# Short-sequence attention on one core: Q and K loaded 32 heads at a time, with the exponential putting the queries back in order

One core of one Trainium2 chip. The metric is device time in microseconds (us), median over runs.

## The reference

```python
batch, n_heads, seq, head_dim = 32, 12, 128, 64          # float32, 384 heads in all
scale = 1.0 / np.sqrt(q.shape[-1])
scores = scale * np.matmul(q, k.transpose(0, 1, 3, 2))
attn = np.exp(scores - np.max(scores, axis=-1, keepdims=True))
attn = attn / (np.sum(attn, axis=-1, keepdims=True) + 1e-8)
return np.matmul(attn, v).astype(np.float32)
```

Inputs are 3 x 12.58 MB, the output 12.58 MB: 50.33 MB must pass between HBM and SBUF whatever the kernel does.

## The kernel before

It works in 24 chunks of 16 heads. GpSimd (POOL) issues the loads, which cast float32 to bf16 on the way (36.70 MB read, 18.35 MB landed); DVE turns Q, K and the output in 32x32 blocks; ACT does the exponential; finished chunks wait nine chunks before ACT issues their stores (`LAG`), so that the loads go first. The parts that matter here:

```python
    TQ = 16; GQ = S // TQ; T = 8; A = 8; CB = 4; NCH = B * H // 16; AHEAD = 7; LAG = 9

    def runs(x, t):
        return x.rearrange("b h (g t) d -> (b h g) (t d)", t=t).rearrange(
            "(n p) x -> p n x", p=128)

    qr, kr, vr, orr = runs(q, TQ), runs(k, TQ), runs(v, T), runs(out, TQ)
    # ... cut ...
    def load_qk(c):
        for src, which in ((qr, 0), (kr, 1)):
            x = pin.tile([128, TQ, D], bf16, tag="qk"[which] + "_bf", name="qk"[which] + "_bf")
            nc.gpsimd.dma_start(out=x, in_=src[:, c, :].rearrange("p (t d) -> p t d", t=TQ))
            chunks[c, which] = x
    # ... cut ...
    def store(c, eng):
        o_sb, _ = osbs.pop(c)
        eng.dma_start(out=orr[:, c, :], in_=o_sb.rearrange("p t d -> p (t d)"))

    e = NCH - 1
    held = {c: [c - LAG] if c >= LAG else [] for c in range(e - 3)}
    held[e - 3] = [e - 12, e - 11, e - 10, e - 9]
    held[e - 2] = [e - 8, e - 7, e - 6]
    held[e - 1] = [e - 5, e - 4, e - 3]
    held[e] = [e - 2, e - 1, e]
    # ... in the loop over chunks, after the work of chunk c:
        for s in held[c]:
            store(s, nc.scalar if s < e - 2 else nc.sync)
```

A chunk's output tile is 128 partitions of 4 KB, and in HBM the chunk is 128 adjacent rows of 4 KB.

The softmax here doesn't subtract the row's maximum and nothing guards it: scores larger than these inputs give would overflow.

## Time and profile before

| | before |
|---|---|
| time | 131.46 us (130.61 to 131.75, 3 runs) |
| profiled span | 129.4 us |
| busy: PE, DVE, ACT, POOL | 56%, 67%, 55%, 61% |
| DMA engines | full in 38 of 40 slices |
| first to last data packet | 126.0 us, for 50.33 MB |

No compute engine is full, and the 16 DMA engines are. The DMA lines of the page are in the prediction below. "Under 512 B" in them counts, in this kernel, packets of 4 bytes: 1344 = 84 x 16, 16 for each DMA. For a DMA from SP or ACT I read this number as the number of engines that carry it.

### The profile page before, as it was taken

The numbers are of one execution on the slowest core, as the hardware profiler recorded it, in microseconds if no ns is written. First come the engines' busy times: TensorE is split into PE (matmuls) and PEld (weight loads), VectorE is DVE, ScalarE is ACT, GpSimd is POOL, SyncE is SP. The second block draws the span as 40 slices with busy tenths as digits, with TensorE's granted clock in tenths as the row PEclk, the third lists the DMA queues.
The fourth block names the chain that finished last, engine by engine and source line by source line (L and its number), as shares of the span: only waits on it lengthen the run. The fifth ranks groups of instructions, "written<-read, shape, count | busy, mean of one in ns | idle before, by whom it ended". The sixth has DMA issues, their size and how long they took to land.

```text
span 129.4 us, 4637 instructions
## 1 busy us (share of the span) xinstructions
PE 72.9 (56%) x2080; PEld 43.6 (34%) x2080; DVE 86.5 (67%) x150; ACT 71.3 (55%) x74; POOL 79.5 (61%) x88
## 2 busy tenths in 40 slices
PE   0049537597746763886622976460977764856000
PEld 0037335334323442354402454220642442535000
DVE  0246576658879697879944589854578999795800
ACT  3219908567948745865760857580637777335000
POOL 6933133335799986998724895909999445553500
PEclk9999976869999999599996579998555999555555
DMA  3999999999999999999999999999999999999991
GB/s 114 275 193 205 209 209 208 208 210 205 211 208 212 204 211 209 209 208 210 282 288 281 208 212 282 288 286 246 250 209 286 236 298 317 405 414 399 412 408 54
DMA packets 16723, 32.27 MB, mean 249 GB/s; under 512 B 1344, under 2 KB 7488, under 8 KB 16704
## 3 DMA queue, kind: packets, MB, share of 16 engines
q0 software_dynamic: 12960, 18.35, 79.8%
q10 hardware_dynamic: 3168, 11.54, 23.0%
q1 hardware_dynamic: 576, 2.10, 4.2%
q8 instruction: 16, 0.26, 0.7%
q14 instruction: 3, 0.02, 0.0%
HBM read 37.75 MB, written 12.58 MB: 389 GB/s over the span
## 4 chain that ended last, share of the span: by engine, by line
DMA 56%; DVE 14%; POOL 11%; PE 9%; issue 2%; ACT 1%; POOLq 0%; DVEq 0%; ACTq 0%
DMA k_bf<-in_k_dram 34%; DMA q_bf<-in_q_dram 11%; DMA v_bf<-in_v_dram 11%; DVE o_sb L178 6%; PE s_ps L120 5%; POOL o_sb L183 4%; POOL v_bf L65 4%; DVE kt L109 3%; PE o_ps L159 3%; DVE qt L107 3%; POOL q_bf L58 2%; ACT attn L124 1%; PE v_ps L139 1%; DVE o_sb L186 1%; POOL k_bf L58 1%
## 5 line engine op out<-in xcount | busy, mean ns | idle before, releaser
L124 ACT ACTIVATE attn<-s_ps 128x2048 bf16<-128x2048 f32 x24 | 45.1, 1879 | 40.6 <-PE s_ps L120 38.5
L183 POOL TENSOR_TENSOR o_sb<-o_sb,recip 128x1024 f32<-128x1024 f32 x23 | 44.0, 1915 | 9.9 <-DVE o_sb L178 9.7
L178 DVE STREAM_TRANSPOSE o_sb<-o_ps 128x512 f32<-128x512 f32 x48 | 33.3, 712 | 15.7 <-PE o_ps L159 14.8
L120 PE MATMUL s_ps<-qt,kt 32*128 32x128 bf16 x768 | 18.6, 245 | 34.2 <-DVE kt L109 34.2
L139 PE MATMUL v_ps<-v_bf,perm 128*32 128x512 bf16 (+1 forms) x448 | 35.0, 418 | 2.7 <-DMA v_bf<-in_v_dram 2.0
L120 PEld LDWEIGHTS <-kt 32*128 32x128 bf16 x768 | 13.8, 106 | 44.2 <-DVE kt L109 44.2
L143 ACT CAST v<-v_ps 128x512 bf16<-128x512 f32 x48 | 26.1, 593 | 2.1 <-PE v_ps L139 2.0
L159 PE MATMUL o_ps<-attn,v 128*32 128x128 bf16 x768 | 22.9, 251 | 1.1 <-issue 1.0
L58 POOL DMA_DIRECT2D k_bf<-in_k_dram x23 | 12.3, 535 | 15.7 <-DMA v_bf<-in_v_dram 11.6
L109 DVE STREAM_TRANSPOSE kt<-k_bf 128x512 f32<-128x512 f32 x24 | 16.4, 684 | 6.2 <-DMA k_bf<-in_k_dram 6.1
L107 DVE STREAM_TRANSPOSE qt<-q_bf 128x512 f32<-128x512 f32 x24 | 16.3, 679 | 5.5 <-DMA q_bf<-in_q_dram 5.4
L159 PEld LDWEIGHTS <-v 128*32 128x32 bf16 x768 | 16.0, 111 | 10.3 <-issue 5.2
L65 POOL DMA_DIRECT2D v_bf<-in_v_dram x12 | 9.3, 778 | 13.0 <-DMA k_bf<-in_k_dram 4.2
L171 DVE STREAM_TRANSPOSE dt<-d_ps 128x512 f32<-128x512 f32 x24 | 16.3, 680 | 1.0 <-PE d_ps L149 1.0
L149 PE MATMUL d_ps<-attn,ones 128*32 128x512 bf16 x96 | 11.2, 453 | 9.0 <-ACT attn L124 8.9
L58 POOL DMA_DIRECT2D q_bf<-in_q_dram x23 | 13.2, 576 | 3.0 <-DMA k_bf<-in_k_dram 1.3
L139 PEld LDWEIGHTS <-perm 128*32 128x32 bf16 x448 | 11.8, 114 | 6.2 <-issue 3.5
L149 PEld LDWEIGHTS <-ones 128*32 128x32 bf16 x96 | 4.4, 103 | 15.4 <-issue 13.2
L173 DVE RECIPROCAL recip<-dt 128x16 f32<-128x16 f32 x24 | 6.1, 254 | 1.9
L83 DVE CAST q_bf<-raw 128x1024 bf16<-128x1024 f32 x1 | 0.7, 694 | 5.5 <-DMA raw<-in_q_dram 5.5
L83 ACT CAST k_bf<-raw 128x1024 bf16<-128x1024 f32 x1 | 1.0, 1045 | 3.2 <-DMA raw<-in_k_dram 3.2
L83 ACT ACT_TABLE_LOAD x1 | 1.3, 1283 | 1.2 <-PEq L243 1.2
(11 smaller groups left out, 3.9 us busy)
## 6 DMA issues: line engine op xcount, KB each, us to landing
out_dram<-o_sb ACTq DMA_DIRECT2D x21, 512.0 KB, 6.8
v_bf<-in_v_dram POOLq DMA_DIRECT2D x12, 512.0 KB, 13.5
q_bf<-in_q_dram POOLq DMA_DIRECT2D x23, 256.0 KB, 12.4
k_bf<-in_k_dram POOLq DMA_DIRECT2D x23, 256.0 KB, 12.4
out_dram<-o_sb SPq DMA_DIRECT2D x3, 512.0 KB, 6.4
raw<-in_k_dram ACTq DMA_DIRECT2D x1, 512.0 KB, 4.9
raw<-in_q_dram SPq DMA_DIRECT2D x1, 512.0 KB, 4.7
```

The lines of the kernel that those rows point to most:

```text
L58: nc.gpsimd.dma_start(out=x, in_=src[:, c, :].rearrange("p (t d) -> p t d", t=TQ))
L107: nc.vector.transpose(xt.rearrange("p h (x g) -> p x h g", g=GQ), x)
L109: nc.vector.transpose(xt.rearrange("p h (x g) -> p x h g", g=GQ), x.rearrange("p (y t) e -> p t y e", y=2))
L120: nc.tensor.matmul(s_ps[:, b, h, :], lhsT=kt[pr, h, :, j], rhs=qt[pr, h, :, j], start=(j == 0), stop=(j == 1), tile_position=(b * 32, 0))
L124: nc.scalar.activation(out=attn, in_=s_ps, func=mybir.ActivationFunctionType.Exp, bias=0.0, scale=scale)
L139: nc.tensor.matmul(v_ps[u * 32:(u + 1) * 32, i], lhsT=perm[:, a + i, tl, :], rhs=v_bf[:, ns, 2 * u + tl, :], start=(tl == 0), stop=(tl == ...
L143: nc.scalar.copy(v2s[m][:, a:a + heads, ns], v_ps)
L149: nc.tensor.matmul(d_ps[b * 32:(b + 1) * 32], lhsT=ones, rhs=attns[c][:, b], start=True, stop=True, tile_position=(0, b * 32))
L159: nc.tensor.matmul(o_ps[b * 32:(b + 1) * 32, h], lhsT=v2s[c // 4][:, 4 * (b % 2) + h, 2 * (c % 4) + b // 2, j * 32:(j + 1) * 32], rhs=attn ...
L171: nc.vector.transpose(dt, turned(d_ps))
L178: nc.vector.transpose(o_sb[:, :, j * 32:(j + 1) * 32], turned(o_ps))
L183: nc.gpsimd.tensor_mul(o_sb, o_sb, recip.to_broadcast([128, TQ, D]))
```

## The change

Its intent: fewer and larger transfers. Q and K come for 32 heads (a "duo" of two chunks) in one DMA, in runs of 8 KB instead of 4 KB, and are turned with one DVE instruction for 32 heads. A partition then holds 32 queries of a head, and the exponential writes its result in another order so that an output row is again 16 queries, 4 KB. The core of the diff:

```diff
-    AHEAD = 7
+    NDUO = NCH // 2
+    AHEAD = 5
-    qr, kr, vr, orr = runs(q, TQ), runs(k, TQ), runs(v, T), runs(out, TQ)
+    qr, kr, vr = runs(q, 2 * TQ), runs(k, 2 * TQ), runs(v, T)
+    orr = out.rearrange("b h s d -> (b h s d)").rearrange(
+        "(m b i p x) -> m i b p x", m=NDUO, b=4, i=2, p=32)
 ...
+    def load_qk(m, which):
+        x = pin.tile([128, 2 * TQ, D], bf16, tag="qk"[which] + "_bf", name="qk"[which] + "_bf")
+        nc.gpsimd.dma_start(
+            out=x, in_=(qr, kr)[which][:, m, :].rearrange("p (t d) -> p t d", d=D))
 ...
+            xt = pt.tile([128, 8, S], f32, tag="qk"[which] + "t", name="qk"[which] + "t")
+            nc.vector.transpose(
+                xt.rearrange("p h (x g) -> p x h g", g=4),
+                x.rearrange("p (y t) e -> p t y e", t=(TQ, T)[which]))
 ...
-                            s_ps[:, b, h, :], lhsT=kt[pr, h, :, j], rhs=qt[pr, h, :, j],
+                            s_ps[:, b, h, :], lhsT=kt[pr, 4 * (c % 2) + h, :, j],
+                            rhs=qt[pr, 4 * (c % 2) + h, :, j],
 ...
-            nc.scalar.activation(out=attn, in_=s_ps, func=mybir.ActivationFunctionType.Exp,
-                                 bias=0.0, scale=scale)
+            nc.scalar.activation(
+                out=attn.rearrange("p b h (x g y) -> p (b h x) g y", g=4, y=2),
+                in_=s_ps.rearrange("p b h (x y g) -> p (b h x) g y", g=4, y=2),
+                func=mybir.ActivationFunctionType.Exp, bias=0.0, scale=scale)
 ...
-                        lhsT=v2s[c // 4][:, 4 * (b % 2) + h, 2 * (c % 4) + b // 2,
+                        lhsT=v2s[c // 4][:, 4 * (c % 2) + h, 4 * (c // 2 % 2) + b,
 ...
-            eng.dma_start(out=orr[:, c, :], in_=o_sb.rearrange("p t d -> p (t d)"))
+            eng.dma_start(out=orr[c // 2, c % 2], in_=o_sb.rearrange("p t d -> p (t d)"))
 ...
-            if c + AHEAD < NCH:
-                load(c + AHEAD)
+            if c % 2 == 0 and c // 2 + 6 < NDUO:
+                load_v(c // 2 + 6)
+            if c // 2 + AHEAD < NDUO:
+                load_qk(c // 2 + AHEAD, c % 2)
```

Cut: the loads ahead of the loop and their order, the first chunk's casts (twice as large), the matching pattern of `perm`, the sizes of the tile pools and the step at which a duo is turned. `store`'s tile in SBUF is the same as before; only its address pattern in HBM is new.

More of the change, by code (lines that the diff above doesn't have):

```diff
@@ L41, in runs @@
             "(n p) x -> p n x", p=128)
-    qr, kr, vr, orr = runs(q, TQ), runs(k, TQ), runs(v, T), runs(out, TQ)
+    qr, kr, vr = runs(q, 2 * TQ), runs(k, 2 * TQ), runs(v, T)
+    orr = out.rearrange("b h s d -> (b h s d)").rearrange(
+        "(m b i p x) -> m i b p x", m=NDUO, b=4, i=2, p=32)
     singles = ctx.enter_context(tc.tile_pool(name="singles", bufs=1))
-    pin = ctx.enter_context(tc.tile_pool(name="pin", bufs=AHEAD + 3))
-    pt = ctx.enter_context(tc.tile_pool(name="pt", bufs=3))
+    pin = ctx.enter_context(tc.tile_pool(name="pin", bufs=AHEAD))
+    pt = ctx.enter_context(tc.tile_pool(name="pt", bufs=2))
     pa = ctx.enter_context(tc.tile_pool(name="pa", bufs=3))
@@ L53 @@
     chunks, qts, attns, v2s, osbs = {}, {}, {}, {}, {}
-    def load_qk(c):
-        for src, which in ((qr, 0), (kr, 1)):
-            x = pin.tile([128, TQ, D], bf16, tag="qk"[which] + "_bf", name="qk"[which] + "_bf")
-            nc.gpsimd.dma_start(out=x, in_=src[:, c, :].rearrange("p (t d) -> p t d", t=TQ))
-            chunks[c, which] = x
+    def load_qk(m, which):
+        x = pin.tile([128, 2 * TQ, D], bf16, tag="qk"[which] + "_bf", name="qk"[which] + "_bf")
+        nc.gpsimd.dma_start(
+            out=x, in_=(qr, kr)[which][:, m, :].rearrange("p (t d) -> p t d", d=D))
+        chunks[m, which] = x
     def load_v(m):
@@ L69 @@
     with tc.manual_schedule():
-        early = {0: 0, 1: 1, 2: 2, 3: 3, 4: 4, 5: 5}
-        early.update({4 * m - 5 + i: 2 * m + i for m in range(3, NCH // 4) for i in range(2)})
-        def load(c):
-            load_qk(c)
-            if c in early:
-                load_v(early[c])
-        for src, which, eng, cast in ((qr, 0, nc.sync, nc.vector.tensor_copy),
-                                      (kr, 1, nc.scalar, nc.scalar.copy)):
-            raw = po.tile([128, TQ, D], f32, tag="o_sb", name="raw")
-            eng.dma_start(out=raw, in_=src[:, 0, :].rearrange("p (t d) -> p t d", t=TQ))
-            x = pin.tile([128, TQ, D], bf16, tag="qk"[which] + "_bf", name="qk"[which] + "_bf")
-            cast(x, raw)
-            chunks[0, which] = x
-        load_v(early[0])
-        load_qk(1)
+        for src, which, eng in ((qr, 0, nc.sync), (kr, 1, nc.scalar)):
+            raw = po.tile([128, 2 * TQ, D], f32, tag="raw", bufs=2, name="raw")
+            eng.dma_start(out=raw, in_=src[:, 0, :].rearrange("p (t d) -> p t d", d=D))
+            chunks[0, which] = raw
+        load_v(0)
+        load_qk(1, 0)
         ident = singles.tile([128, 128], bf16)
         make_identity(nc, ident)
-        load_v(early[1])
+        load_qk(1, 1)
+        load_v(1)
         perm = singles.tile([128, A, 2, 32], bf16)
@@ L93, with turn @@
             nc.vector.tensor_copy(
-                perm[:, :, tl, tl * 16:(tl + 1) * 16].rearrange("p a (x g) -> p a x g", x=2),
-                ident.rearrange("p (a g x) -> p a x g", a=A, x=2))
+                perm[:, :, tl, tl * 16:(tl + 1) * 16].rearrange("p a (x g) -> p a x g", x=4),
+                ident.rearrange("p (a g x) -> p a x g", a=A, x=4))
         ones = singles.tile([128, 32], bf16)
         nc.vector.memset(ones, 1.0)
-        for c in range(2, AHEAD):
-            load(c)
-        def turn(c, which):
-            x = chunks.pop((c, which)).bitcast(f32)
-            xt = pt.tile([128, 4, S], f32, tag="qk"[which] + "t", name="qk"[which] + "t")
-            if which == 0:
-                nc.vector.transpose(xt.rearrange("p h (x g) -> p x h g", g=GQ), x)
-            else:
-                nc.vector.transpose(xt.rearrange("p h (x g) -> p x h g", g=GQ),
-                                    x.rearrange("p (y t) e -> p t y e", y=2))
-            qts[c, which] = xt.bitcast(bf16).rearrange("p h (s j) -> p h s j", j=2)
+        for which in range(2):
+            raw = chunks[0, which]
+            x = pin.tile([128, 2 * TQ, D], bf16, tag="qk"[which] + "_bf", name="qk"[which] + "_bf")
+            nc.vector.tensor_copy(x[:, :TQ], raw[:, :TQ])
+            nc.scalar.copy(x[:, TQ:], raw[:, TQ:])
+            chunks[0, which] = x
+        for m in range(2, AHEAD):
+            if m == 3:
+                load_v(3)
+            load_qk(m, 0)
+            load_qk(m, 1)
+            if m == 2:
+                load_v(2)
+            if m == 3:
+                load_v(4)
+                load_v(5)
+        def turn(m, which):
+            x = chunks.pop((m, which)).bitcast(f32)
+            xt = pt.tile([128, 8, S], f32, tag="qk"[which] + "t", name="qk"[which] + "t")
+            nc.vector.transpose(
+                xt.rearrange("p h (x g) -> p x h g", g=4),
+                x.rearrange("p (y t) e -> p t y e", t=(TQ, T)[which]))
+            qts[m, which] = xt.bitcast(bf16).rearrange("p h (s j) -> p h s j", j=2)
         def scores(c):
-            qt, kt = qts.pop((c, 0)), qts.pop((c, 1))
+            qt, kt = qts[c // 2, 0], qts[c // 2, 1]
             s_ps = ps.tile([128, 4, 4, S], f32, tag="s_ps", name="s_ps")
@@ L210 @@
             todo = shuffles.get(c, [])
-            if c < e:
-                turn(c + 1, 0)
-                turn(c + 1, 1)
+            if c < e - 1:
+                turn(c // 2 + 1, c % 2)
             d_ps = denominators(c)
```

## The prediction

In the prediction and the expectations, k is the number of DMA engines that carry a DMA. That the store, with 4 as its slowest dimension in HBM, gets k = 4 is assumed there (the "rule on k"): the kernel before has 16 small packets for every DMA and doesn't show it. "Engines 0 to 3", "0 to 7" and "0 and 1" are only names for the engines that carry the stores, "4 to 15" for the rest.

> **What bounds the kernel now.** I read the strip of 40 slices first, then the DMA queues, the chain of work that ended last, the costliest groups, and the packet records of the trace. From the page of the kernel before:
>
> ```profile
> DMA  3999999999999999999999999999999999999991
> GB/s 114 275 193 205 209 209 208 208 210 205 211 208 212 204 211 209 209 208 210 282 288 281 208 212 282 288 286 246 250 209 286 236 298 317 405 414 399 412 408 54
> DMA packets 16723, 32.27 MB, mean 249 GB/s; under 512 B 1344, under 2 KB 7488, under 8 KB 16704
> ...
> q0 software_dynamic: 12960, 18.35, 79.8%
> q10 hardware_dynamic: 3168, 11.54, 23.0%
> q1 hardware_dynamic: 576, 2.10, 4.2%
> ...
> HBM read 37.75 MB, written 12.58 MB: 389 GB/s over the span
> ...
> DMA 56%; DVE 14%; POOL 11%; PE 9%; issue 2%; ACT 1%; POOLq 0%; DVEq 0%; ACTq 0%
> ```
>
> The 16 DMA engines are full from the second slice to the last but one. The GB/s row counts what lands; the casting loads land bf16, half of what they read. So 208 in slices 4 to 18, when only loads run, is 416 GB/s read, and 405 to 414 at the end, when only stores run, is the same rate. Counting the source bytes in the packet records confirms this: 411.6 GB/s over the stretch of loads alone, 407.0 where loads and stores mix, 397.2 over the last stores. The size of a piece hardly matters: two-microsecond stretches of almost only v pieces (2 KB read, 1 KB landed) run at 401 to 418, of only q/k pieces (4 KB read, 2 KB landed) at 405 to 424, of only stores (4 KB) at 391 to 426. So the kernel is bound by bytes per DMA engine: 50.33 MB / 16 engines = 3.146 MB each. First to last data packet is 126.0 us, and they begin about 3.4 us into the 129.4 us span. The timed run is 131.46 us, 2 us more than the profiled span.
>
> No compute engine comes close, and the groups that the change touches are these (busy us, mean ns | idle before):
>
> ```profile
> L124 ACT ACTIVATE attn<-s_ps 128x2048 bf16<-128x2048 f32 x24 | 45.1, 1879 | 40.6 <-PE s_ps L120 38.5
> L58 POOL DMA_DIRECT2D k_bf<-in_k_dram x23 | 12.3, 535 | 15.7 <-DMA v_bf<-in_v_dram 11.6
> L109 DVE STREAM_TRANSPOSE kt<-k_bf 128x512 f32<-128x512 f32 x24 | 16.4, 684 | 6.2 <-DMA k_bf<-in_k_dram 6.1
> L107 DVE STREAM_TRANSPOSE qt<-q_bf 128x512 f32<-128x512 f32 x24 | 16.3, 679 | 5.5 <-DMA q_bf<-in_q_dram 5.4
> ...
> out_dram<-o_sb ACTq DMA_DIRECT2D x21, 512.0 KB, 6.8
> ```
>
> DVE is busy 67% and the exponential, the largest group of ACT, sits idle 40.6 us before its instructions. A store of 512 KB lands in 6.8 us beside other traffic. Stores begin at 57.9 us, since each is held back nine chunks.
>
> [...] 58 casting loads, 22 DMAs on q10 and 4 on q1, each with 16 small packets, make 84 x 16 = 1344, which is exactly the count "under 512 B". A smaller k isn't shown by the kernel before.
> [...]
>
> **The change part by part.**
>
> *Q/K loads.* 46 casting DMAs of 128 pieces become 22, and the two first uncast ones double to 1 MB. In the packet records a 1 KB landed piece takes 98 ns and a 2 KB one 173 ns, so 75 ns per KB and 23 ns fixed; a 4 KB one is then, as an estimate, 23 + 4 x 75 = 323 ns instead of 2 x 173 = 346. In packet time that is 5888 x 173 = 1019 us against 2816 x 323 = 910 us, plus about 40 us more in the first raw loads: 69 us / 16 = 4 us at the very most. But packet times of one queue overlap (their sum is 107.7% of 16 engines' span) and the rate in bytes is the same for both sizes, so I count 0 to 1 us. The 24 fewer DMAs save 24 x 16 x 20 ns / 16 = 0.5 us of small packets.
>
> *POOL issues.* 46 x 0.555 us = 25.5 us becomes about 22 x 0.555 = 12.2 us: 13 us less on an engine that feeds a queue which is never empty. Worth 0.
>
> *Turns.* 48 DVE transposes of 512 elements at 0.68 us = 32.7 us become 24 of 1024. From the recorded 670 ns minimum[...], one takes 1.2 us, so 28.9 us: 3.8 us less on DVE, which isn't the bound. Worth 0.
>
> *Exponential.* Same 2048 elements, contiguous output, read out of order from PSUM: 1.88 us each. Even 20% more would be 9 us against 40 us of idle time. Worth 0. The first chunk's casts double (0.69 + 1.05 us more) and wait for 2 MB instead of 1 MB, about 2.6 us later: hidden behind the loads in flight.
>
> *Stores.* Here is the term that I let decide. A chunk now holds heads 4i to 4i+3 of each of four groups of eight. The output pattern goes from 128 rows of 4 KB in one even step to 4 blocks, 256 KB apart, of 32 adjacent rows of 4 KB. The blocks can't be merged with the rows, as the other chunk's 128 KB lies between them. The runs stay 4 KB, but the slowest dimension in HBM is now 4 instead of 128. [...] The loads (128 rows outermost) still use all 16.
>
> Work of each of engines 0 to 3: loads 37.75 MB / 16 = 2.359 MB, stores 12.58 MB / 4 = 3.146 MB, together 5.505 MB. One engine moves 407 / 16 = 25.4 GB/s in the mixed part. 5.505 MB / 25.4 GB/s = 216.5 us. Engines 4 to 15 have 2.359 MB, 93 us, and idle for the rest. Are engines 0 to 3 busy throughout? Until the first store at about 58 us they carry loads as now; from then one store is 131 KB / 25.4 GB/s = 5.2 us on them, plus 98 KB / 25.4 = 3.9 us of a chunk's loads, 9.0 us, while the compute produces a chunk in less than 5 us. Stores pile up, and with 12 output tiles and a lag of nine about three stores stand in the queue when the loop stalls for a free output tile. So they don't run dry. The path is: 3.4 us to the first packet, some 1 us for the ramp, 216.5, and the last receipt, about 0.5 us: 221.4 us span; with the 2 us between span and timed run 223.4. Four engines alone could go nearer to their shortest packet, 159 ns for 4 KB (25.8 GB/s), which takes about 2 us off. I predict 222 us.
>
> **The rivals.**
> *A: the store still uses all 16 engines* [...]. For it: stores come through today on 16 engines. [...] Then bytes per engine are unchanged, nothing else is on the path, and the time is 129 to 133 us.
> *B: larger pieces raise the DMA rate.* For it: 23 ns fixed per packet[...]. Against it: equal bytes per second for 1, 2 and 4 KB pieces in the records. With 16-engine stores, at most 4 + 0.5 us: about 127 us, faster by over 2%.
> *C: k is 4 but the four engines change from store to store.* For it: nothing in this profile tells engines apart. [...] Then the bytes even out, a store merely takes longer to land, and the time is 130 to 138 us.
> *D: k is 4, and engines 0 to 3 also run dry* while the loop waits for an output tile or for loads slowed on those four. For it: a store needs 9 us beside loads[...]. Against it: twelve output tiles and ten chunks of loads in flight. It would add 5 to 15 us: 227 to 237.
>
> **Range and chances.** I hold the rule on k at a little over 0.8[...]. Within it, 25.8 GB/s with perfect filling gives 218, rates a little higher on four engines alone about 210, and rival D up to 238. I don't stretch the range over the gap to A and B: 207 to 238. Slower by over 2%: 0.83 (k = 4, and a little of C). Same: 0.13 (A, part of C). Faster: 0.04 (B).
>
> **What would show each step right or wrong.** Right: "under 512 B" falls to 34 x 16 + 2 x 16 + 24 x 4 = 672; with 16-engine stores it would be 960. The GB/s row falls from about 58 us on and ends at about 100, a quarter of 408, over more than 50 us, with the DMA row at 2 or 3 tenths. A store's time to landing rises from 6.8 us to well over 10. The chain of waits names the output transfer, and DVE or POOL wait for it. Turns x24 at about 1.2 us, exponential at 1.88 us. The rate before the first store stays near 208 landed: if it rises above 215, the step on piece size is wrong. A DMA row of nines to the end, or 960 small packets, makes the whole prediction wrong.

## The result, and the profile after

| | before | after |
|---|---|---|
| time, median | 131.36 us (130.61 to 131.75, 4 runs) | 218.41 us (217.91 to 218.98, 4 runs) |
| profiled span | 129.4 us | 216.1 us |
| first to last data packet | 126.0 us | 212.7 us |

The ratio is 1.664 (95% interval 1.655 to 1.673). Ratios here are the mean time of one kernel's fast runs over that of the other's fast runs of the same rounds, so not quite the ratio of the medians quoted. Executions over 1.5% slower than the fastest of the same kernel are left out of the means.

The strip of 40 slices and the DMA queues of the kernel after, the counterpart of the first fence in the prediction:

```profile
DMA  6999999999999999952222222222222222222221
GB/s 220 274 205 218 203 216 204 213 213 210 210 213 237 231 230 244 234 128 83 77 71 71 101 109 105 109 105 106 108 106 105 106 105 106 105 106 105 106 105 67
DMA packets 12979, 32.80 MB, mean 152 GB/s; under 512 B 672, under 2 KB 6816, under 8 KB 12704
...
q0 software_dynamic: 9504, 17.83, 44.3%
q10 hardware_dynamic: 2916, 12.06, 13.9%
q1 hardware_dynamic: 540, 2.62, 3.2%
```

The slices are 5.4 us now. Until slice 17, at 92 us, all 16 engines are full, as before, for the loads still keep the other twelve busy. Then the row of nines drops to 2 tenths for half the kernel, and the rate to 105 to 106 GB/s. Four engines out of 16 are 25%, and 105 / 4 = 26.3 GB/s for each, against 407 / 16 = 25.4 in the mixed part of the kernel before: full speed for four engines, nothing for twelve. The small packets have fallen to 672 = 34 x 16 (casting loads) + 2 x 16 (first loads) + 24 x 4 (stores): four for each store. Slices 19 to 22 show less than 105 only because some loads, which land half of what they read, still run on the same four engines; counted by source bytes that stretch is at 99 to 105 GB/s.

The groups that the change touched (busy us, mean ns of one | idle before), and the issues of the stores:

```profile
L133 ACT ACTIVATE attn<-s_ps 128x2048 bf16<-128x2048 f32 x24 | 45.0, 1877 | 88.2 <-PE s_ps L128 51.1
L116 DVE STREAM_TRANSPOSE qt<-q_bf 128x1024 f32<-128x1024 f32 x12 | 14.5, 1209 | 1.4 <-DMA q_bf<-in_q_dram 1.4
L116 DVE STREAM_TRANSPOSE kt<-k_bf 128x1024 f32<-128x1024 f32 x12 | 14.4, 1203 | 0.0
L62 POOL DMA_DIRECT2D k_bf<-in_k_dram x11 | 6.4, 578 | 10.0 <-DMA v_bf<-in_v_dram 4.3
...
out_dram<-o_sb ACTq DMA_DIRECT2D x21, 512.0 KB
```

Everything that the change set out to make cheaper is as cheap as hoped. The exponential costs the same out of order (1877 against 1879 ns), 24 turns of 1.2 us replace 48 of 0.68, and half as many issues take half as long. The store's line has lost its last number: the profile gives no time to landing for these stores.

Three more views of the kernel after: the chain of waits, one line of the list of all waits (total us, times, longest us), and the timeline near the end (start us, duration us, what; an "x4" spans four instructions):

```profile
ACTq 8%; DVE 1%; ACT 1%; PE 0%; issue 0%; DVEq 0%
```

```profile
DVE o_sb L189 <- DMA out_dram<-o_sb: 42.3, 10, 11.0
```

```profile
137.22 15.70 ACTq L202 DMA_DIRECT2D out_dram<-o_sb  x4
148.61 35.23 SPq L202 DMA_DIRECT2D out_dram<-o_sb  x3
153.02 1.88 ACT L133 ACTIVATE attn<-s_ps 128x2048 bf16<-128x2048 f32 x1 [14.00 <-issue]
153.10 24.07 ACTq L202 DMA_DIRECT2D out_dram<-o_sb  x3
177.28 1.88 ACT L133 ACTIVATE attn<-s_ps 128x2048 bf16<-128x2048 f32 x1 [22.38 <-issue]
```

Issuing a store, normally half a microsecond (median 0.565 us), took up to 14.4 us: ACT sat in its issue, for what the trace doesn't show, and the exponential behind it in the same program order came 22 us late. DVE, too, waited 42.3 us for stores to leave output tiles free. This chain covers only some 10% of the span, a sign that it has lost the track: it stops at an issue that began at 160.5 us and doesn't show what that issue waited for. Read alone it would point to ACT as the culprit. E3 tests that.

### The profile page after: what moved, and what is told of

Its sections match the earlier page's. It is cut to its first block, busy times and chain, and to the rows that moved or that the text cites. A ratio compares the mean times of both kernels' runs of the same rounds, so it can differ in the third digit from the quotient of the medians.

```text
span 216.1 us, 4593 instructions
## 1 busy us (share of the span) xinstructions
PE 76.4 (35%) x2080; PEld 45.2 (21%) x2080; DVE 83.0 (38%) x127; ACT 73.0 (34%) x75; POOL 67.1 (31%) x64
## 5 line engine op out<-in xcount | busy, mean ns | idle before, releaser
L133 ACT ACTIVATE attn<-s_ps 128x2048 bf16<-128x2048 f32 x24 | 45.0, 1877 | 88.2 <-PE s_ps L128 51.1
L189 DVE STREAM_TRANSPOSE o_sb<-o_ps 128x512 f32<-128x512 f32 x48 | 32.3, 699 | 56.4 <-DMA out_dram<-o_sb 42.3
L150 PE MATMUL v_ps<-v_bf,perm 128*32 128x512 bf16 (+1 forms) x448 | 37.4, 440 | 9.8 <-DMA v_bf<-in_v_dram 8.8
L182 DVE STREAM_TRANSPOSE dt<-d_ps 128x512 f32<-128x512 f32 x24 | 16.4, 682 | 32.4 <-PE d_ps L160 32.2
L128 PE MATMUL s_ps<-qt,kt 32*128 32x128 bf16 x768 | 19.1, 244 | 26.8 <-DVE kt L116 26.3
L170 PEld LDWEIGHTS <-v 128*32 128x32 bf16 x768 | 17.0, 115 | 12.6 <-issue 8.5
L150 PEld LDWEIGHTS <-perm 128*32 128x32 bf16 x448 | 13.0, 117 | 12.4 <-issue 9.7
L116 DVE STREAM_TRANSPOSE qt<-q_bf 128x1024 f32<-128x1024 f32 x12 | 14.5, 1209 | 1.4 <-DMA q_bf<-in_q_dram 1.4
L116 DVE STREAM_TRANSPOSE kt<-k_bf 128x1024 f32<-128x1024 f32 x12 | 14.4, 1203 | 0.0
L62 POOL DMA_DIRECT2D q_bf<-in_q_dram x11 | 5.9, 540 | 17.6 <-DMA v_bf<-in_v_dram 7.5
L62 POOL DMA_DIRECT2D k_bf<-in_k_dram x11 | 6.4, 578 | 10.0 <-DMA v_bf<-in_v_dram 4.3
L197 POOL TENSOR_TENSOR o_sb<-o_sb,recip 128x512 f32<-128x512 f32 x1 | 1.0, 1044 | 21.2 <-issue 21.2
L97 ACT CAST q_bf<-raw 128x1024 bf16<-128x1024 f32 x1 | 1.0, 1045 | 6.3 <-DMA raw<-in_q_dram 6.3
```

The lines of the kernel that those rows point to most:

```text
L62: nc.gpsimd.dma_start(out=x, in_=(qr, kr)[which][:, m, :].rearrange("p (t d) -> p t d", d=D))
L116: nc.vector.transpose(xt.rearrange("p h (x g) -> p x h g", g=4), x.rearrange("p (y t) e -> p t y e", t=(TQ, T)[which]))
L128: nc.tensor.matmul(s_ps[:, b, h, :], lhsT=kt[pr, 4 * (c % 2) + h, :, j], rhs=qt[pr, 4 * (c % 2) + h, :, j], start=(j == 0), stop=(j == 1), ...
L133: nc.scalar.activation(out=attn.rearrange("p b h (x g y) -> p (b h x) g y", g=4, y=2), in_=s_ps.rearrange("p b h (x y g) -> p (b h x) g y" ...
L150: nc.tensor.matmul(v_ps[u * 32:(u + 1) * 32, i], lhsT=perm[:, a + i, tl, :], rhs=v_bf[:, ns, 2 * u + tl, :], start=(tl == 0), stop=(tl == ...
L170: nc.tensor.matmul(o_ps[b * 32:(b + 1) * 32, h], lhsT=v2s[c // 4][:, 4 * (c % 2) + h, 4 * (c // 2 % 2) + b, j * 32:(j + 1) * 32], rhs=attn ...
```

## The experiments

My theory: the store's outermost dimension of 4 puts all output through four DMA engines, and nothing else in the change matters. Rivals: blocks with gaps in HBM are slow in themselves; the 8 KB loads or the new order of compute cost the time; ACT's long issues do.

### E5 to E8: the kernel before, with only the store's pattern changed

One edit, with K = 4, 8, 16, 2. The rows land in the wrong places, so the result is wrong; the work and the bytes are the same.

```diff
-    qr, kr, vr, orr = runs(q, TQ), runs(k, TQ), runs(v, T), runs(out, TQ)
+    qr, kr, vr = runs(q, TQ), runs(k, TQ), runs(v, T)
+    orr = out.rearrange("b h s d -> (b h s d)").rearrange(
+        "(m b i p x) -> m i b p x", m=NCH // 2, b=K, i=2, p=128 // K)
-            eng.dma_start(out=orr[:, c, :], in_=o_sb.rearrange("p t d -> p (t d)"))
+            eng.dma_start(out=orr[c // 2, c % 2], in_=o_sb.rearrange("p t d -> p (t d)"))
```

> The kernel before with nothing changed but the store's address pattern in HBM: 4 blocks of 32 rows with gaps (rows land in the wrong places: a wrong result on purpose). Theory: the pattern alone makes the loss; engines 0 to 3 carry 2.359 + 3.146 = 5.505 MB at 25.4 to 26.4 GB/s, 214 to 222 us; small packets 928 + 64 of the raw loads and their queue's share as before and 24 x 4 = 96 for stores, 1056 in all. Rival (loads of 8 KB or the compute's new order share in it): under 200 us.

> The same with 8 blocks of 16 rows (wrong result on purpose). Theory: k = 8; engines 0 to 7 carry 2.359 + 1.573 = 3.932 MB, 149 to 155 us of transfer plus 6 to 7 us: 156 to 162 us. Rival (any gap in the pattern costs the same, or more blocks cost more): 218 us or more.

> The same with 16 blocks of 8 rows (wrong result on purpose). Theory: k = 16; the gaps cost nothing, 130 to 133 us, like the kernel before. Rival (gaps in HBM are the cost): slower than e6.

> The same with 2 blocks of 64 rows (wrong result on purpose). Theory: k = 2; engines 0 and 1 carry 2.359 + 6.291 = 8.650 MB, 328 to 341 us of transfer plus 6 to 7 us: 334 to 348 us. Rival (fewer, larger blocks are better for HBM): under 218 us.

| K | MB on the fullest engine | expected us | measured us | first to last data packet | GB/s of that engine | small packets |
|---|---|---|---|---|---|---|
| 2 | 8.650 | 334 to 348 | 339.06 | 333.8 us | 25.9 | 1008 |
| 4 | 5.505 | 214 to 222 | 220.12 | 215.1 us | 25.6 | 1056 |
| 8 | 3.932 | 156 to 162 | 160.99 | 155.5 us | 25.3 | 1152 |
| 16 | 3.146 | 130 to 133 | 133.16 (3 fast runs) | 127.5 us | 24.7 | 1344 |
| before | 3.146 | | 131.56 in those rounds | 126.0 us | 25.0 | 1344 |

The small packets are 928 + 32 + 24 K in every row (my text for E5 says 64 for the first loads where it is 32; its sum of 1056 was right). The GB/s rows of K = 8 and K = 2, the two profiles in turn:

```profile
GB/s 167 220 207 210 207 208 206 208 210 207 209 209 210 209 207 233 256 259 259 266 244 158 193 158 161 258 223 157 151 158 173 212 209 209 210 210 196 211 209 56
```

```profile
GB/s 198 201 208 208 209 209 208 219 220 179 96 73 116 38 95 45 104 49 53 54 52 55 53 52 52 53 52 52 54 53 52 52 52 53 52 52 52 53 52 40
```

The end plateau is about 210 for K = 8, 105 for K = 4 and 52 for K = 2: 26.2 to 26.3 GB/s per engine each time. So one line, the address pattern of the store, makes the whole loss. Bytes on the fullest engine at one rate, 25.6 GB/s, plus about 5 us before, after and outside the profiled span, give the times for K = 2, 4 and 8 within 1.5%; for K = 16 they give 128, 4% too little. Gaps in HBM as the cause of the loss are out: K = 16 has the most gaps and is nearly as fast as before. Nearly: 1.0177 (1.009 to 1.026), with fast runs from 132.70 to 134.50 us, at the edge of what I expected; by the record's limit of 2% its verdict is "unclear". The average packet of its last stores took 173 ns against 162 before (and 172 in E11, which has the same blocks), so 16 blocks of 32 KB with gaps seem a little slower to write than one run of 512 KB. Why, no run here shows.

### E3: all stores from SP

```diff
-                store(s, nc.scalar if s < e - 2 else nc.sync)
+                store(s, nc.sync)
```

> The changed kernel with all stores issued from SP instead of ACT and SP; still 4 blocks. Theory (engines 0 to 3 are full from the first store on): 216 to 220 us, though ACT no longer sits behind the issue of stores (22 us before one exponential in the changed kernel). Rival (the long issues of stores on ACT hold up the compute and so the end): 190 to 210 us.

Measured: correct, 219.8 us. The waits are quite other ones. The issues of the stores (ns min/median/max, first and last start us), and two lines of the list of waits:

```profile
L202 SPq DMA_DIRECT2D out_dram<-o_sb x24: 529/4726/13087, 32.7 to 193.1; - x24
```

```profile
ACT v L154 <- PE v_ps L150: 57.6, 16, 16.5
PE v_ps L150 <- DMA v_bf<-in_v_dram: 55.5, 6, 17.4
```

The first store is issued from SP at 32.7 us, where ACT issued it at 62.0 us, and the longest waits are now for V tiles, not ACT's for its own queue. The time is nearly the same. ACT's long issues were a symptom: with four engines full to the end, it doesn't matter which engine waits.

### E1: the same change with 16 blocks

The duo's heads are shared out to its two chunks alternately, instead of four and four of each eight. Then the block (4) and head (4) dimensions merge into one of 16.

```diff
-        "(m b i p x) -> m i b p x", m=NDUO, b=4, i=2, p=32)
+        "(m b i p x) -> m i b p x", m=NDUO, b=16, i=2, p=8)
 ...
-                            s_ps[:, b, h, :], lhsT=kt[pr, 4 * (c % 2) + h, :, j],
-                            rhs=qt[pr, 4 * (c % 2) + h, :, j],
+                            s_ps[:, b, h, :], lhsT=kt[pr, 2 * h + c % 2, :, j],
+                            rhs=qt[pr, 2 * h + c % 2, :, j],
 ...
-                        lhsT=v2s[c // 4][:, 4 * (c % 2) + h, 4 * (c // 2 % 2) + b,
+                        lhsT=v2s[c // 4][:, 2 * h + c % 2, 4 * (c // 2 % 2) + b,
```

> The changed kernel with the chunk's heads taken as 2h+i of each eight instead of 4i+h, so that the store's pattern is 16 blocks of 8 rows instead of 4 blocks of 32 rows; everything else as changed; right result. Theory [...]: k = 16, small packets 960 instead of 672, DMA row full to the end, 127 to 132 us. Rival (scattered blocks of a store are slow in themselves, or the 8 KB loads or the reordered exponential cost the time): stays above 200 us. If 8 KB loads do raise the rate (the changed kernel read about 2% more per us before its first store), it beats 131.4 by 1 to 3 us.

Measured: correct, 136.15 us, 960 small packets. The indices in four places bring back 82 us. But 136.15 is 1.036 (1.032 to 1.041) of before, and not the 127 to 132 us that I expected. Its strip, and one line each of its timeline and its waits (total us, times, longest us):

```profile
DMA  4999999999999999999999999999999859999992
GB/s 100 411 240 208 196 216 207 205 218 206 206 218 208 215 212 207 217 202 216 261 300 227 276 217 286 274 284 287 215 215 254 238 154 229 378 363 324 379 400 94
```

```profile
96.67 0.59 ACT L154 CAST v<-v_ps 128x512 bf16<-128x512 f32 x1 [6.75 <-PE v_ps L150]
```

```profile
PE v_ps L150 <- DMA v_bf<-in_v_dram: 16.4, 4, 7.3
```

ACT stood still 6.75 us before 96.67 us, for a V tile whose load took 30 us to land behind Q and K loads issued before it for later chunks. Some 10 us later (slices 32 to 34: 8, 5, 9) the loads were through, the compute was late, and the held stores weren't there yet: DMA engines idle, which is time lost for good in a kernel bound by them. E10 and E11 follow from this.

### E2 and E9: each store cut into four DMAs of 32 partitions

E2 cuts the stores of the changed kernel, E9 those of the kernel before, which go to one run of 512 KB.

```diff
-            eng.dma_start(out=orr[c // 2, c % 2], in_=o_sb.rearrange("p t d -> p (t d)"))
+            for b in range(4):
+                eng.dma_start(out=orr[c // 2, c % 2, b],
+                              in_=o_sb[b * 32:(b + 1) * 32].rearrange("p t d -> p (t d)"))
```

> The changed kernel with each store cut into four DMAs, one for each block of 32 rows; right result. Theory: each has an outermost dimension of 32, so k = 16; small packets 544 + 32 + 96 x 16 = 2112; 128 to 134 us, a little above e1 because 75 more DMAs are issued on ACT. Rival (4 KB runs 256 KB apart are the cost): stays near 218 us, since the bytes go to the same places.

> The kernel before with each store cut into four DMAs of 32 partitions, to the same contiguous 512 KB in HBM; right result. It asks why e2 needed 150.9 us where 128 to 134 was expected. Theory: DMAs of 32 partitions are slow in themselves, wherever they write ([...] e2's 4 KB packets took 237 ns instead of 162): 145 to 155 us, DMA row not full over the last stores. Rival (the 128 KB blocks with gaps in HBM are the cost): 131 to 134 us.

E2: correct, 150.87 us; 2112 small packets as expected, 16 for each DMA, so I take all 16 engines to be in use, and yet 17 us above my range. E9: correct, 148.0 us. Since E9 has no gaps in HBM, gaps aren't the reason in E2; cutting the stores is. The strip of E9:

```profile
DMA  4999999999999999999999999999998499658374
GB/s 135 235 203 210 204 209 211 207 206 211 206 210 208 209 209 210 228 275 278 258 208 266 265 278 264 241 230 275 278 304 274 106 245 258 184 141 253 112 198 124
```

From the last load's end to the last packet, with only stores left, E9 moves 195 GB/s and E2 194, where the kernel before moves 381. A 4 KB packet takes 236 and 237 ns on average instead of 162. Two things are mixed in these rates. Packets are slower: in E9 34% of them took 290 to 400 ns, about twice the usual 159, against 0.2% in the kernel before. And engines stand idle: they are busy 70% of that stretch against 94% before, and in both runs the exponential waited up to 11 us behind the issue of several short DMAs. Why the packets are slower isn't shown: no run here separates the 32 partitions of a DMA from the mere number of DMAs.

### E4: the stores issued by GpSimd

```diff
-                store(s, nc.scalar if s < e - 2 else nc.sync)
+                store(s, nc.gpsimd)
```

> The changed kernel with all stores issued from GpSimd; still 4 blocks. [...] bytes even out over 16 engines, 130 to 150 us, small packets 544 + 32 + 24 x 16 = 960. Rival [...]: near 218 us.

That the bytes even out when GpSimd issues the stores was assumed and not shown by an earlier run; the rival is that the same four engines carry every store, whoever issues it. Measured: correct, 173.64 us, between the two and 24 us above my range. The same four engines can't have carried all stores, or the time would be near 218, as in E3 (219.8). The strip and the packet count:

```profile
DMA  5999999999999999999999964434445899998630
GB/s 172 355 208 199 219 204 214 208 208 213 212 207 216 205 218 206 214 215 214 259 266 271 230 144 113 138 80 114 123 108 132 130 212 238 232 227 227 161 126 22
DMA packets 22483, 32.83 MB, mean 192 GB/s; under 512 B 10176, under 2 KB 16320, under 8 KB 22208
```

That agrees with four engines which change from store to store, but the trace doesn't name engines. What I missed: in slices 24 to 31 only some four tenths of the engines are busy, a store takes 16.4 us to land, and DVE waits 35.3 us for output tiles to come free, which suggests that in this kernel's order too few stores are in flight to keep 16 engines full. And the 10176 small packets are not 960: 9216 more, which is 384 for each of the 24 stores. What these are, and what they cost, isn't settled.

### E10, E11, E12: V and the stores timed for the larger loads

E10 is E1 with V loaded when the kernel before loads it; E11 is E10 with the held stores let go sooner; E12 is the kernel before with E11's stores.

```diff
-            if c % 2 == 0 and c // 2 + 6 < NDUO:
-                load_v(c // 2 + 6)
+            if c % 4 < 2 and 2 * (c // 4) + 6 + c % 4 < NDUO:
+                load_v(2 * (c // 4) + 6 + c % 4)
```

```diff
-        held = {c: [c - LAG] if c >= LAG else [] for c in range(e - 3)}
-        held[e - 3] = [e - 12, e - 11, e - 10, e - 9]
-        held[e - 2] = [e - 8, e - 7, e - 6]
-        held[e - 1] = [e - 5, e - 4, e - 3]
+        held = {c: [c - LAG] if c >= LAG else [] for c in range(e - 7)}
+        held.update({c: [2 * c - 25, 2 * c - 24] for c in range(e - 7, e)})
         held[e] = [e - 2, e - 1, e]
```

> e1 with the V loads issued at the steps at which the kernel before issues them (the odd half one step sooner and the even and odd halves in successive steps); right result. Theory: in e1 the compute stood still from 90 to 96 us for a V tile that took 30 us to land, and the engines then ran out of stores (154 GB/s in one slice): with it gone 131 to 134 us. If the 8 KB loads' higher rate (about 430 against 412 GB/s) pays too, 129 to 131. Rival (the last 3 us of e1 are due to the pattern of 16 blocks alone, as in e7): stays at 135 to 136.

> e10 with the held stores let go two in each step from chunk 16 on, instead of four, three, three and three at the end; right result. Theory: the DMA engines don't run dry when the loads are through, 128 to 131 us, a little faster than the kernel before. Rival (the engines were already full at that time, so that earlier stores only hold up the loads): same as e10 or slower.

> The kernel before with only the release of the held stores spread as in e11 (two in each step from chunk 16 on); right result. It asks whether e11's gain over the kernel before belongs to the 8 KB loads or to the spread. Theory (the 8 KB loads' higher rate is the gain; the kernel before has its DMA row at nine to the end, so a spread frees nothing): 130.5 to 132 us, same as before. Rival (the spread is the gain): 129 to 130 us.

E10: correct, 134.41 us, 1.7 us better than E1, but a little above the 131 to 134 that I expected of mere recovery; the late V tile was only part of E1's loss. Its DMA row still has a hole, in slice 33:

```profile
DMA  4999999999999999999999999999999979999990
```

E11: correct, 129.97 us, 0.991 of before (0.988 to 0.994). E12: correct, 131.31 us, 0.999 (0.994 to 1.004): the spread alone does nothing for the kernel before. E11's strip:

```profile
DMA  4999999999999999999999999999999999999991
GB/s 86 418 252 216 204 216 216 199 212 219 199 211 220 200 214 213 212 210 213 210 276 281 245 278 278 287 260 246 282 216 242 275 338 398 428 367 357 396 330 42
```

The hole is gone. So the change without its store pattern, and with V and the stores timed for it, is worth 1%. The loads-only stretch reads 415.9 GB/s in E11 against 411.0 before: for the 35.65 MB that GpSimd loads in E11, 85.7 instead of 86.7 us, about what was gained. That this is the cause is consistent, not isolated: the profiled run of E11 was its slowest, 131.00 us, and its first to last data packet took 125.8 us against 126.0 before; E11's stores also run through the 16 blocks, which seem slightly slower.

## Why the prediction was right, point by point

**What bounds the kernel**: right. Runs in which the fullest engines stay full end where bytes per engine put them, within 1.5% for K = 2, 4 and 8 and within 4% for 16. E1, E2 and E9 lose time where the strip shows engines not full; in E2 and E9 slower packets come on top.

**Four engines for a store**: right, to the packet (672), and the plateau at a quarter of the rate (105 GB/s against 405 to 414). Which four they are isn't in the trace; that they are always the same follows from the time, since stores that spread over 16 engines could not take this long (E1 took 136.15 us). The count of 84 x 16 in the kernel before shows less than it seems: only the 26 DMAs from SP and ACT in it bear on k, since in E4 the same 4 blocks, stored by GpSimd, left 400 small packets each and not four.

**The sum**: 216.5 us of transfer plus 1 us of ramp stood against a measured 212.7 from first to last packet. The term that was a little off is the rate: I took 25.4 GB/s from the mixed stretch of the kernel before, and four engines alone moved 26.3 during stores. Every packet there took 159 ns, but one began every 155.5 ns, so they overlap a little; I had taken 159 ns (25.8 GB/s) for the least spacing, and named a correction of about 2 us for it. It was 4 to 5, and 222 became 218.4. The 3.4 us to the first packet were misread as well: it comes at 1.7 us, and the rest lies after the last one; that changes the sum by about half a us.

**Engines 0 to 3 stay busy** (against rival D): right. The GB/s row holds 105 without a gap to the end.

**Turns, exponential, issues**: right in size (1.20 us predicted and 1.21 measured; 1.88 and 1.88; 12.2 us and 12.3) and right in being worth nothing here; the 1.20 us of a turn and the cost of the exponential out of order were estimates, which the kernel before doesn't show. The second 512 elements of a turn cost 0.53 us (0.68 to 1.21), less than a turn of their own.

**Loads**: right in sum, not in its reason. I said that the size of a piece doesn't change the rate. A fit over 1 us stretches of the loads before the first store gives 427 GB/s for the 8 KB reads after against 414 for the 4 KB reads before, 3% more. Over all loads before the first store that is 415.7 against 411.0 GB/s, within the 0 to 1 us that I counted. Rival B was thus a little true, and E11 shows about a quarter of its 4.5 us.

**Rival A, 16-engine stores, 129 to 133 us**: not quite. E1, this very case, took 136.15, because the coarser loads upset the timing of V and of the stores. I had put nothing on the path there but bytes. **Rival C, changing engines, 130 to 138 us**, erred the same way: E4, whose stores seem to behave like that, took 173.64.

**Signs to look for**: the small packets, the plateau and the rows of turns and exponential came as written, and DVE did wait for the output (42.3 us). The GB/s row fell at 92 us and not at 58, since the loads kept the other twelve engines busy until then; the prediction's own 93 us for these engines said as much. The time to landing wasn't given, and the chain of waits named ACT's issue, not the transfer; both signs were badly chosen.

## What to carry to other kernels

Before changing the address pattern of a DMA from SP or ACT, write down its slowest dimension: with 2, 4 or 8 there, that many engines carried it all here, and the time from first to last data packet was the bytes on the fullest engine at 25.3 to 25.9 GB/s. Here a relabelling of what goes where (which heads form a chunk) made that dimension 16 and brought back 82 us, where cutting the DMA into narrow ones brought back 68. In this kernel, bound by transfers, the larger loads needed the load order and the release of stores tuned again, and the row of DMA slices showed where they weren't.
